# RWKV systems in two PSUM banks, TensorE's order beside r, v and z written out by hand, mixed inputs in other slots, next weights handed over

## The chip, the cores and the metric

The kernel runs on one core of one Trainium2 chip. The metric is the device time of one execution in microseconds (us); the time of a kernel is the median over several executions. Engines are named as in the profile: PE is TensorE (PEld its weight loads), DVE is VectorE, ACT is ScalarE, POOL is GpSimd, SP is the engine whose queue issues the DMAs.

## The reference

One inference step of two layers over 1104 tokens (8 sequences of 8, 16 meta tokens, 1024 of a prompt) with 1024 channels, all in fp32. Layer 0 is a gated DeltaNet, layer 1 RWKV-7 time mixing. The change lies in layer 1, in what comes before its recurrence:

```
xx = xprev - xn
xs = xn[None] + xx[None] * mu[:, None, None, :]
rkvz = jnp.einsum('sbtd,sde->sbte', xs[:4], w_rkvz)
...
kk = l2norm((k * k_k).reshape(B, T, H, N))
...
S = (S * d_t[:, :, None, :]
     + jnp.einsum('bhvk,bhk->bhv', S, -kk_t)[..., None] * b_t[:, :, None, :]
     + v_t[..., None] * k_t[:, :, None, :])
```

So every one of r, k, v, z is a 1024 x 1024 projection of its own mixture of a token and the token before it. The kernel does the recurrence in chunks of 64 tokens; for each chunk and head the effect of the kk and b terms is a lower triangular system, whose inverse it needs. Those inverses need only k, the decay and the rate a, so that they can be worked out while r, v and z are still being projected.

## The kernel before, in words

**Stages of layer 1.** First keys, decays and rates (`keys_decay_rate`, L1134: for each of 8 output tiles k the key projection, then two small second projections, `lora_second`). Then the stage of the change (`layer1`, L1861): 24 projections in the order r, v, z with 8 output tiles of 128 channels each, and beside them 24 systems in 5 batches. Then `wave` (L1905), which runs the recurrence over 24 items with the last third of the tokens' z projection, the output projection and the last norm beside it.

**A projection.** The tokens lie in three segments of 384, 384 and 336 (`SEGS`). Operands are split in two parts, high and low, so that a product takes three matmuls (high x high, low weight x high, high weight x low). One segment of one output tile is 8 input tiles x 3 = 24 matmuls into one PSUM tile (`dense`, L236, tag "d", 4 buffers). ACT copies the result out (L1131; for z ACT and DVE gate it, L1003) and SP stores it. r and v take three segments, z two; the third of z waits for the wave.

**Weights.** `load_w` (L195) loads half an output tile's weights, 4 x 128 x 128, as `wraw` (2 buffers); `split` (L82) then has ACT write the high part `whi` (L86) and POOL the low part `wlo` (L90). whi and wlo have three buffers each, and a projection holds two of them, so that the second half of the next projection can be split only when the first half of this one has been read for the last time, after matmul 12 of 24 of its last segment.

**Mixed inputs.** For each of r, v and z, `mix` has `mix_part` (L1028) make 8 input tiles x its segments: `mix_raw` (L1032) is one ACT and one DVE instruction (two each in the first segment), then ACT writes the high part and, for odd k POOL, for even k DVE, the low part (L90). They lie in 11 slots: r in 0 to 5, 9, 10, v in 6, 7, 8, 0, 1, 2, 9, 10, z in 3 to 10. The keys before used 3 to 10. So for v three of the slots are free beforehand, and the rest are freed by the last projection of r, segment by segment. The names of the tiles in the profile are xa, xc, xh and xl; they show the slot, not the part.

**Systems.** `rwkv_inverse` (L1272) does one batch of 4 or 5 items. For each item: a load (`sldcak`), three ACT functions (two exponentials, a square), three products (L1290 and L1296 on DVE, L1295 on POOL), 48 small matmuls into `fL` and 8 into `frss`, copied out by ACT (L1306, L1308) and a DVE transpose (L1322). For the batch: `inverse32` (L457) builds a 32 x 32 inverse in each partition, 31 steps of two DVE instructions (L470, L472) of 31 to 256 elements each, in the SBUF tile `invT` that POOL has zeroed (L461) and given its diagonal (L465). Two DVE transposes (L1336 `T1n`, L1337 `sTD`) follow. Then for each item `merge_left` (24 small matmuls into `mY`, two ACT copies L484) and `merge_right` (24 into `mU`, two ACT copies); both take PSUM tag "m", two buffers. At last the batch is stored (L1344).

**What sets the order.** The queue of each engine is written by a planner when the program is built: it takes the instructions as far as possible in the order in which they are traced and by its own estimate of when their inputs are ready. Once written, a queue is executed in order. In `layer1` projections and batches are traced one after the other (batches after projections 0, 3, 6, 9, 12), and the planner alone puts the small matmuls of the systems between those of the projections. The wave stands in `manual_schedule` for PE and ACT, which keeps the traced order on these. Its weights come from `stream` (L217), which keeps up to six halves loaded ahead and three split.

## Time and profile before

| what | us |
|---|---|
| time, median of 3 | 2294.88 (2293.03 to 2296.75) |
| the profiled execution's own time | 2294.9 |
| its span, first to last instruction | 2293.2 |
| PE busy in the span | 2142.2 (93%) |
| DVE busy | 1591.0 (69%) |
| ACT busy | 1270.4 (55%) |
| POOL busy | 926.3 (40%) |

How to read it: the span is 1.7 us shorter than the execution that it belongs to. The stage of the change is the stretch from about 1481 us, where r's projections begin in earnest, to about 1860 us, where the wave's first matmuls (`zz`) begin. A row of "windows" gives a stretch, its length, then for PE, PEld, DVE, ACT and POOL the busy time and in brackets the number of instructions, then the granted TensorE clock (1.00 is full), the busy share of the DMA engines and GB/s. A row of groups gives line, engine, operation, tiles and shape, the count, the busy time of the group and the mean duration of one in ns, then the idle time before them and what ended it. A row of waits gives who waited for whom: total us, number of times, longest. Neighbouring matmuls overlap in the records, so that what counts is the distance from start to start.

### The profile page before, as it was taken

The numbers are of one execution on the slowest core, as the hardware profiler recorded it, in microseconds if no ns is written. First come the engines' busy times: TensorE is split into PE (matmuls) and PEld (weight loads), VectorE is DVE, ScalarE is ACT, GpSimd is POOL, SyncE is SP. The second block draws the span as 40 slices with busy tenths as digits, with TensorE's granted clock in tenths as the row PEclk, the third lists the DMA queues.
The fourth block names the chain that finished last, engine by engine and source line by source line (L and its number), as shares of the span: only waits on it lengthen the run. The fifth ranks groups of instructions, "written<-read, shape, count | busy, mean of one in ns | idle before, by whom it ended". The sixth has DMA issues, their size and how long they took to land. (4 is left out here: it accounts for less than half of the span.)

```text
span 2293.2 us, 55145 instructions
## 1 busy us (share of the span) xinstructions
PE 2142.2 (93%) x20452; PEld 1957.5 (85%) x20452; DVE 1591.0 (69%) x4222; ACT 1270.4 (55%) x3638; POOL 926.3 (40%) x1263
## 2 busy tenths in 40 slices
PE   5989999989999999999999998999889899999997
PEld 5888988989898998988998998898778888888786
DVE  6878769585868769586334765768977737776655
ACT  5445556555555556465534464664744436677674
POOL 3435344443434344443321352364533444444444
PEclk9999999999999999999999999999989999999999
DMA  4324232323334232335435225565444375677754
GB/s 117 101 77 109 75 96 79 104 83 88 102 90 108 67 105 73 102 89 156 122 89 156 72 63 188 194 201 155 149 140 135 90 212 156 192 212 228 226 164 143
DMA packets 430663, 292.66 MB, mean 128 GB/s; under 512 B 147146, under 2 KB 412987, under 8 KB 430395
## 3 DMA queue, kind: packets, MB, share of 16 engines
q1 hardware_dynamic: 430394, 289.14, 44.1%
q8 instruction: 161, 2.64, 0.5%
q14 instruction: 108, 0.88, 0.1%
HBM read 197.68 MB, written 91.37 MB: 126 GB/s over the span
## 5 line engine op out<-in xcount | busy, mean ns | idle before, releaser
L90 POOL TENSOR_TENSOR wlo<-wraw,whi 128x512 fp32r<-128x512 f32 (+1 forms) x246 | 325.5, 1326 | 379.1 <-ACT whi L86 366.9
L76 PE MATMUL d<-xc,whi 128*128 128x384 f32 (+2 forms) x910 | 263.7, 346 | 4.7 <-DVE key L1187 2.3
L86 ACT CAST whi<-wraw 128x512 fp32r<-128x512 f32 (+1 forms) x246 | 150.2, 613 | 105.1 <-PE dq L76 50.6
L434 DVE SCALAR_TENSOR_TENSOR cvy<-raw,cw,cvy 128x408 f32<-128x408 f32 (+2 forms) x288 | 179.4, 636 | 16.3 <-ACT cvy L62 14.5
L76 PEld LDWEIGHTS d<-xc,whi 128*128 128x128 f32 (+1 forms) x910 | 171.2, 195 | 12.0 <-issue 3.9
L472 DVE TENSOR_TENSOR invT<-invT,invtmp 72x31 f32<-72x31 f32 (+31 forms) x403 | 174.1, 432 | 6.7
L470 DVE TENSOR_TENSOR invtmp<-invA,invT 72x31 f32<-72x31 f32 (+31 forms) x403 | 164.4, 408 | 12.2 <-DMA invA<-ltd 5.4
L76 PE MATMUL dz<-xc,whi 128*128 128x384 f32 (+1 forms) x480 | 149.8, 343 | 0.0
L76 PE MATMUL dv<-xc,whi 128*128 128x384 f32 (+1 forms) x480 | 146.7, 335 | 0.0
L76 PE MATMUL d<-xc,wlo 128*128 128x384 f32 (+2 forms) x428 | 146.2, 347 | 0.2
L76 PE MATMUL d<-xa,whi 128*128 128x384 f32 (+3 forms) x450 | 140.6, 346 | 2.3 <-DVE xa L90 0.9
L834 POOL TENSOR_SCALAR Sb<-Sb,eglb 128x128 f32<-128x128 f32 x128 | 80.1, 643 | 88.2 <-DMA Sb<-in_state_gdn 43.8
L76 PE MATMUL dz<-xa,whi 128*128 128x384 f32 (+1 forms) x288 | 101.5, 352 | 0.0
L76 PE MATMUL dv<-xa,whi 128*128 128x384 f32 (+1 forms) x288 | 100.4, 349 | 0.1
L76 PEld LDWEIGHTS dz<-xc,whi 128*128 128x128 f32 x480 | 90.1, 193 | 0.8
L76 PEld LDWEIGHTS d<-xa,whi 128*128 128x128 f32 (+1 forms) x450 | 84.5, 192 | 6.7 <-issue 2.4
L76 PEld LDWEIGHTS dv<-xc,whi 128*128 128x128 f32 x480 | 88.5, 188 | 0.5 <-issue 0.4
L76 PE MATMUL d<-xl,whi 128*128 128x384 f32 (+1 forms) x256 | 84.7, 347 | 3.2 <-DVE xl L90 1.7
L62 ACT ACTIVATE o<-rA,gcol 128x128 f32<-128x128 f32 x128 | 46.6, 372 | 73.2 <-DVE S L745 72.5
L76 PE MATMUL d<-xh,wlo 128*128 128x384 f32 (+1 forms) x256 | 85.0, 346 | 1.7 <-POOL wlo L90 1.7
L76 PE MATMUL d<-xa,wlo 128*128 128x384 f32 (+3 forms) x252 | 85.6, 340 | 0.0
L62 ACT ACTIVATE attn<-attn,gcol 128x128 f32<-128x128 f32 x144 | 46.5, 390 | 70.2 <-POOL attn L545 70.1
(518 smaller groups left out, 7022.9 us busy)
## 6 DMA issues: line engine op xcount, KB each, us to landing
wraw<-in_gdn_w_in SPq DMA_DIRECT2D x96, 256.0 KB
wraw<-in_rwkv_w_rkvz SPq DMA_DIRECT2D x80, 256.0 KB
Sb<-in_state_gdn SPq DMA_DIRECT2D x64, 256.0 KB
sldcak<-cakd SPq DMA_DIRECT2D x24, 576.0 KB
cakd<-ev SPq DMA_DIRECT2D x56, 192.0 KB
wraw<-in_rwkv_w_o SPq DMA_DIRECT2D x42, 256.0 KB
E<-drow SPq DMA_DIRECT2D x24, 384.0 KB
attn<-drow SPq DMA_DIRECT2D x24, 384.0 KB
```

The lines of the kernel that those rows point to most:

```text
L62: return self.nc.scalar.activation(out, in_, func, bias=bias, scale=scale, **kw)
L76: self.nc.tensor.matmul(out, lhsT, rhs, start=start, stop=stop)
L86: nc.scalar.copy(hi, x)
L90: e.tensor_tensor(lo, x, hi.bitcast(F32), op=ALU.subtract)
L434: nc.vector.scalar_tensor_tensor(y[:, 0:wd], raw[:, k:k + wd], cw[k], y[:, 0:wd], op0=ALU.mult, op1=ALU.add)
L470: nc.vector.tensor_tensor(tmp, A[:, j, j + 1:32].unsqueeze(2).broadcast_to([nb, n, m]), Tv[:, j, 0:m].unsqueeze(1).broadcast_to([nb, n, m] ...
L472: nc.vector.tensor_tensor(Tv[:, j + 1:32, 0:m], Tv[:, j + 1:32, 0:m], tmp, op=ALU.subtract)
L834: nc.gpsimd.tensor_scalar(Sb[:, u], Sb[:, u], self.eglb[:, hv, 4 * g + u:4 * g + u + 1], None, op0=ALU.mult)
```

## The change

- **The inverse grows in PSUM.** `inverse_steps` replaces `inverse32` for these five batches: the tile T of 128 x 1024 lies in PSUM (tag "T", one buffer, as wide as two of the 512-wide PSUM tiles) in place of SBUF, DVE zeroes it and writes the diagonal in place of POOL, and after each of the 31 steps the generator yields. With it tag "d" has 3 buffers in place of 4 in this stage and tag "m" 1 in place of 2, and the PSUM pool is opened anew after the keys.
- **TensorE's order is written out.** The stage stands in `manual_schedule` for PE. `projections` yields after every 8 matmuls: 64 segments x 3 = 192 places. What is to be traced at a place stands in `plan`: item n's small matmuls (`lower`) and the loads and products of item n + 1 (`prepare`) at place `LOWER[n]`; the steps of batch b's inverse spread over the places up to `END[b]`; the left merge of its item q at `END[b] + 2 + 3q`, the right merge two places later. The other engines stay with the planner.
- **Mixed inputs in other slots.** r takes slots 0, 1, 3 to 7, 2; v 8, 9, 10, 0, 1, 3, 4, 2; z 5 to 10, 3, 4. `free` says how many of a projection's first inputs lie in slots that the projections before it do not use: 2 for r, 3 for v and z. Those are mixed during keys 2 to 4 (r) or tiles 4 to 6 of the matrix before (v, z), the others behind each segment of its last tile; for this the last tile of the keys is done segment by segment. The first tile of a matrix begins with the matmuls of its free inputs for all segments and then returns to finish each segment. All low parts are made by POOL.
- **Next weights handed over.** The weights of the next projection are loaded half by half, behind the first and the last segment. The wave's first z tile finds its weights split (projection 24 in `weights`) and those of the second loaded (`raws`); `stream` takes both.

No matmul is added or left out. The diff, without parts that only move or repeat lines:

```diff
-    def stream(self, srcs):
-
-        raw, w = [], []
+    def stream(self, srcs, first, loaded):
+
+        raw, w = [None] * len(first) + loaded, list(first)
         for n in range(len(srcs)):
-            while len(raw) < min(n + 6, len(srcs)):
+            while len(raw) < min(n + 6 - (n == 1), len(srcs)):
                 q = len(raw)
                 if q > 2 and len(w) < q - 2:
                     x, m, c = raw[len(w)]
                     hi, lo = (self.t(self.wp, [128, 4, 128], a, 3, F32R) for a in ("whi", "wlo"))
                     self.split(x[:, 0:m, 0:c], hi[:, 0:m, 0:c], lo[:, 0:m, 0:c])
...
-                raw.append(self.load_w(srcs[q], srcs[q].shape[0] // 128, later=True, pool=self.fin if q % 3 == 2 else None))
-            while len(w) < min(n + 3, len(srcs)):
+                raw.append(self.load_w(srcs[q], srcs[q].shape[0] // 128, later=True, pool=self.fin if q % 3 == 1 else None))
+            while len(w) < min(n + 3 - (n == 1), len(srcs)):
...
-        p = self.ps("m", 2, "Y")
+        p = self.ps("m", 1, "Y")
...
-        p = self.ps("m", 2, "U")
+        p = self.ps("m", 1, "U")
...
-    def mix_part(self, m, k, a, b, xb, xh, xl, pool):
+    def mix_part(self, m, k, a, b, xb, xh, xl, pool, lo=None):
         x = self.mix_raw(m, k, a, b, xb, pool)
-        self.split(x, xh[:, a:b], xl[:, a:b], eng_lo="pool" if k % 2 else "dve")
+        self.split(x, xh[:, a:b], xl[:, a:b], eng_lo=lo or ("pool" if k % 2 else "dve"))
...
-                for (c0, n), p in zip(SEGS, self.projected(1, k, x, k in (0,))):
+                for s, ((c0, n), p) in enumerate(zip(SEGS, self.projected(1, k, x, k in (0, 7)))):
...
+                    if k == 7:
+                        behind(s)
                 self.lora_second(0, k, hh, w2, dst_w)
                 self.lora_second(1, k, hl, w2, dst_a)
+                between(k)
 
...
-    def rwkv_inverse(self, b, pool):
-
-        items = range(max(5 * b - 1, 0), 5 * b + 4)
+    def inverse_steps(self, A, pool, diag, e):
+
+        self.uid += 1
+        T = self.pp.tile([128, 1024], F32, name=f"invT_{self.uid}", tag="T", bufs=1)
+        self.nc.vector.memset(T, 0.0)
+        self.nc.vector.tensor_copy(T[:, 0:1024:33], diag)
+        Tv = T.rearrange("p (i j) -> p i j", j=32)
+        for j in range(31):
+            n, m = 31 - j, j + 1
+            tmp = self.t(pool, [128, 256], "invtmp", 1)[:, 0:n * m].rearrange("p (n m) -> p n m", m=m)
+            e.tensor_tensor(tmp, A[:, j, j + 1:32].unsqueeze(2).broadcast_to([128, n, m]),
+                            Tv[:, j, 0:m].unsqueeze(1).broadcast_to([128, n, m]), op=ALU.mult)
+            e.tensor_tensor(Tv[:, j + 1:32, 0:m], Tv[:, j + 1:32, 0:m], tmp, op=ALU.subtract)
+            yield
+        return Tv
+
+    def inverse_plan(self, pool):
+
         nc, t = self.nc, self.t
-        rk2, L21, GD, TD = self.rk2[:, b], self.L21[b % 2], self.GD, self.TD
-        for q, n in enumerate(items):
+        keep = {}
+        GD, TD = self.GD, self.TD
+
+        def prepare(n):
             s, p = divmod(n, 8)
-            C = slice(6 * q, 6 * q + 6)
...
+            keep[n] = sq, bk, al
+
+        def lower(b, q, n):
+            s, p = divmod(n, 8)
+            sq, bk, al = keep.pop(n)
+            C = slice(6 * q, 6 * q + 6)
+            rk2, L21 = self.rk2[:, b], self.L21[b % 2]
             gp = self.ps("f", 2, "L")
...
+        def chain(b):
+            rk2 = self.rk2[:, b]
+            nc.vector.reciprocal(rk2, rk2)
+            blk = t(pool, [128, 32], "bblk", 1)
+            nc.vector.transpose(blk, rk2)
+            A = t(pool, [128, 32, 32], "invA", 1)
+            flat = lambda x: x.rearrange("p a b -> p (a b)")
+            nc.vector.transpose(flat(A), flat(GD))
+            nc.vector.tensor_tensor(A, A, blk.unsqueeze(2).broadcast_to([128, 32, 32]), op=ALU.mult)
+            Tv = yield from self.inverse_steps(A.rearrange("p i s -> p s i"), pool, blk, nc.vector)
+            T1n = t(pool, [128, 32, 32], "T1n", 1)
+            if b == 0:
+                for a in (32, 96):
+                    nc.gpsimd.memset(TD[a:a + 32, :, 1, :], 0.0)
+            nc.vector.transpose(T1n.rearrange("p c j -> p j c"), Tv.rearrange("p i j -> p j i"))
+            nc.vector.transpose(TD[:, :, 0, :].rearrange("p c i -> p i c"), Tv)
+            keep["T", b] = T1n
+        def left(b, q):
             C = slice(6 * q, 6 * q + 6)
-            self.merge_right(self.merge_left(L21[:, C], T1n[:, C], pool), TD[:, C])
-        w = 6 * len(items)
-        d = self.ttd[b].rearrange("s (c x i) -> s c x i", x=2, i=32)[:, 0:w]
-        for a in (0, 64):
-            nc.sync.dma_start(d[a:a + 32], TD[a:a + 32, 0:w])
-            for x in (0, 1):
-                nc.sync.dma_start(d[a + 32:a + 64, :, x], TD[a + 32:a + 64, 0:w, 1 - x])
+            keep["Y", b, q] = self.merge_left(self.L21[b % 2][:, C], keep["T", b][:, C], pool)
+        def right(b, q):
+            self.merge_right(keep.pop(("Y", b, q)), TD[:, 6 * q:6 * q + 6])
+        def store(b, items):
+            w = 6 * len(items)
+            d = self.ttd[b].rearrange("s (c x i) -> s c x i", x=2, i=32)[:, 0:w]
+            for a in (0, 64):
+                nc.sync.dma_start(d[a:a + 32], TD[a:a + 32, 0:w])
+                for x in (0, 1):
+                    nc.sync.dma_start(d[a + 32:a + 64, :, x], TD[a + 32:a + 64, 0:w, 1 - x])
+        return prepare, lower, chain, left, right, store
...
-        self.keys_decay_rate(x, self.hh, self.hl)
+        todo = [(m, k) for m in (0, 2, 3) for k in range(8)]
+        order = {0: (0, 1, 3, 4, 5, 6, 7, 2), 2: (8, 9, 10, 0, 1, 3, 4, 2), 3: (5, 6, 7, 8, 9, 10, 3, 4)}
+        free = {0: 2, 2: 3, 3: 3}
+        segs = {0: 3, 2: 3, 3: 2}
+        lows = {0: "pool", 2: "pool", 3: "pool"}
+        W = {}
+        def part(m, k, s):
+            c0, n = SEGS[s]
+            self.mix_part(m, k, c0, c0 + n, xb[k], *self.slots[order[m][k]], self.ev, lows[m])
+        def weights(n, h, elo=None):
+            if n < 25:
+                m, k = (todo + [(3, 0)])[n]
+                (hi,), (lo,) = self.load_w(self.i["rwkv_w_rkvz"][0, m][512 * h:512 * h + 512, 128 * k:128 * k + 128], 4, elo=elo)
+                W[n, h] = hi, lo
+        def between(k):
+            if k in (2, 3, 4):
+                for q in range(free[0]):
+                    part(0, q, k - 2)
+        def behind(s):
+            if s != 1:
+                weights(0, s // 2)
+            for q in range(free[0], 7):
+                part(0, q, s)
+        self.keys_decay_rate(x, self.hh, self.hl, between, behind)
+        for s in range(3):
+            part(0, 7, s)
+        self.psum_pool()
         ip = pool("rinv", ctx)
         self.rwkv_masks(ip, True)
-        todo = [(m, k) for m in (0, 2, 3) for k in range(8)]
-        slots = {0: (0, 1, 2, 3, 4, 5, 9, 10), 2: (6, 7, 8, 0, 1, 2, 9, 10), 3: range(3, 11)}
-        for n, (m, k) in enumerate(todo):
-            if k == 0:
-                x = self.mix(m, xb, slots[m], SEGS[0:2] if m == 3 else SEGS)
-            self.project(m, k, x, {0: self.rd, 2: self.vd, 3: self.zd}[m], k in range(8))
-            if n in (0, 3, 6, 9, 12):
-                self.rwkv_inverse((0, 3, 6, 9, 12).index(n), ip)
-            if n == 16:
-                zin = self.gate_inputs(xa, xb)
+        prepare, lower, chain, first_, second_, store = self.inverse_plan(ip)
+        plan = {}
+        at = lambda u, f, *a: plan.setdefault(u, []).append((f, a))
+        LOWER = (13, 17, 21, 25, 29, 33, 38, 43, 48, 53, 60, 67, 73, 79, 85, 90, 95, 100, 104, 110, 118, 126, 134, 142)
+        DUR, END = (0,), (49, 80, 105, 143, 170)
+        runs = [[chain(b), 0] for b in range(5)]
+        def pump(b, f):
+            while runs[b][1] < f:
+                runs[b][1] += 1
+                next(runs[b][0], None)
+        at(0, prepare, 0)
+        for b in range(5):
+            items = range(max(5 * b - 1, 0), 5 * b + 4)
+            for q, n in enumerate(items):
+                at(LOWER[n], lower, b, q, n)
+                if n < 23:
+                    at(LOWER[n], prepare, n + 1)
+            u0 = LOWER[items[-1]] + 1
+            if b:
+                u0 = max(u0, END[b - 1] + 1)
+            for u in range(u0, END[b] + 1):
+                at(u, pump, b, 99 if u == END[b] else 33 * (u + 1 - u0) / (END[b] + 1 - u0))
+            for q in range(len(items)):
+                at(END[b] + 2 + 3 * q, first_, b, q)
+                at(END[b] + 2 + 3 * q + 2, second_, b, q)
+            at(END[b] + 2 + 3 * q + 2, store, b, items)
+        def projections():
+            for n, (m, k) in enumerate(todo):
+                ps = {}
+                f = free[m] if k == 0 else 0
+                for first, s in [(True, s) for s in range(segs[m] if f else 0)] + [(False, s) for s in range(segs[m])]:
+                    c0, w = SEGS[s]
+                    if s not in ps:
+                        ps[s] = self.ps("d", 3)
+                    p = ps[s]
+                    for c in range(0 if first else 3 * f, 3 * f if first else 24):
+                        q, j = divmod(c, 3)
+                        xh, xl = self.slots[order[m][q]]
+                        hi, lo = W[n, q // 4]
+                        l, r = ((hi, xh), (lo, xh), (hi, xl))[j]
+                        self.mm(p[:, 0:w], l[:, q % 4], r[:, c0:c0 + w], start=c == 0, stop=c == 23)
+                        if c % 8 == 7 and c < 23:
+                            yield
+                    if first:
+                        continue
+                    late = b_now[0] in ()
+                    if s == 0:
+                        weights(n + 1, 0, "dve" if late else None)
+                    if s == segs[m] - 1:
+                        weights(n + 1, 1, "dve" if late else None)
+                    f_ = t(self.ev, [128, 384], "ev", 3)
+                    if m == 3:
+                        self.gate(f_[:, 0:w], p[:, 0:w])
+                    else:
+                        nc.scalar.copy(f_[:, 0:w], p[:, 0:w])
+                    nc.sync.dma_start({0: self.rd, 2: self.vd, 3: self.zd}[m][k][:, c0:c0 + w], f_[:, 0:w])
+                    nm = {0: 2, 2: 3}.get(m)
+                    if nm:
+                        if 4 <= k < 7 and k - 4 < segs[nm]:
+                            part(nm, s, k - 4)
+                        if k == 7 and s < segs[nm]:
+                            for q in range(free[nm], 8):
+                                part(nm, q, s)
+                    yield
+        b_now = [-1]
+        t = self.t
+        with tc.manual_schedule(engines={mybir.EngineType.PE}):
+            for u, _ in enumerate(projections()):
+                b_now[0] = max([b for b in range(5) if u > LOWER[max(5 * b + 3, 0)]], default=-1)
+                for f, a in plan.pop(u, ()):
+                    f(*a)
+                if u == 146:
+                    zin = self.gate_inputs(xa, xb)
+            raws = [self.load_w(self.i["rwkv_w_rkvz"][0, 3][512 * h:512 * h + 512, 128:256], 4, later=True) for h in (0, 1)]
+            for u in sorted(plan):
+                for f, a in plan.pop(u):
+                    f(*a)
...
-            self.wave(zin, stay, last, pool)
+            self.wave(zin, [W[24, h] for h in (0, 1)], raws, stay, last, pool)
```

25 lines of the change are left out of this document (5 added, 20 removed).

## Prediction

> **What bounds the kernel now.** First the windows by stage: the stage of the change and the wave's first 15 us.
>
> ```profile
> 1481.00:1860.00 379.00, 345.30 (x4019) 317.59 (x4020) 291.89 (x548) 200.25 (x490) 164.02 (x224) 0.93 0.51 153
> 1860.00:1875.00 15.00, 11.62 (x62) 10.37 (x61) 2.76 (x7) 4.23 (x9) 5.98 (x5) 0.77 0.75 218
> ```
>
> TensorE bounds the stage: 345.3 of 379 us busy, 33.7 idle. Its granted clock is 0.93 there. What that costs is seen in the chain (22 matmuls of z at full clock, the row before them 21 behind a gap) in two narrow windows, and in the gap between these from the timeline.
>
> ```profile
> 1816.57 5.01 PE d L76 x21
> 1822.37 4.06 PE d L76 x22
> ...
> 1622.00:1625.00 3.00, 3.00 (x19) 3.00 (x18) 2.93 (x8) 2.17 (x6) 1.05 (x3) 1.00 0.53 163
> 1628.00:1631.00 3.00, 3.00 (x53) 2.40 (x45) 2.96 (x7) 1.68 (x4) 2.03 (x3) 0.50 0.49 182
> 1627.73 1.06 PE L76 MATMUL fL<-sldcak 64*32 64x64 f32 x41 [2.37 <-issue]
> ```
>
> A matmul takes 0.185 us at full clock (4.06 / 22). The clock is 1.00 or 0.50; the first window lies ahead of the gap of 2.37 us, the second behind it. A mean of 0.93 is half clock for 14% of the stage (0.07 / 0.5), and 14% of 345.3 busy us, at half speed, lose 24 us. So the same matmuls without a gap would take 379 - 33.7 - 24 = **321 us**, and each us of gap costs 0.71 us more in clock (24 / 33.7).
>
> Then the waits of TensorE, 1481 to 1870 us:
>
> ```profile
> PE fL L76 <- DVE sldcak L1296: 11.0, 8, 2.4
> PE mY L76 <- DVE T1n L1336: 6.8, 3, 3.1
> PE zz L76 <- DVE zst L1003: 3.2, 1, 3.2
> PE fL L76 <- ACT sldcak L62: 2.8, 2, 1.5
> PE fL L76 <- issue: 2.4, 1, 2.4
> PE mU L76 <- ACT invY L484: 2.0, 3, 0.9
> ```
>
> Most of the gaps, 25.0 us in the five rows of fL, mY and mU, stand before small matmuls of the systems, which the planner put where their inputs were not ready yet, mostly behind DVE. That leaves 8.7 of 33.7 for all else. Why DVE is late is seen in its timeline, with POOL's row of the same time below:
>
> ```profile
> 1801.98 1.48 DVE L470 TENSOR_TENSOR invtmp<-invA,invT 128x220 f32<-128x220 f32 x1
> 1803.50 1.35 DVE L472 TENSOR_TENSOR invT<-invT,invtmp 128x220 f32<-128x220 f32 x1
> 1804.89 0.37 DVE L470 TENSOR_TENSOR invtmp<-invA,invT 128x207 f32<-128x207 f32 x1
> ...
> 1801.61 3.00 POOL L90 TENSOR_TENSOR wlo<-wraw,whi 128x512 fp32r<-128x512 f32 x2 [1.53 <-issue]
> ```
>
> While POOL splits weights, a step of the inverse takes 1.4 us; the next, hardly smaller, takes 0.37.
>
> **Part 1, the inverse in PSUM.** One view gives minimum, median and maximum of the steps, the mixing (both tensors in SBUF) and the gate (one in PSUM); the group rows give totals.
>
> ```profile
> L470 DVE TENSOR_TENSOR invtmp<-invA,invT x155: 176/374/1548, 1536.5 to 1813.2; 128x31 f32<-128x31 f32 x10, 128x60 f32<-128x60 f32 x10, 128x87 f32<-128x87 f32 x10, 128x112 f32<-128x112 f32 x10
> L470 DVE TENSOR_TENSOR invtmp<-invA,invT 128x31 f32<-128x31 f32 (+15 forms) x155 | 70.1, 453 | 4.0
> L472 DVE TENSOR_TENSOR invT<-invT,invtmp 128x31 f32<-128x31 f32 (+15 forms) x155 | 73.8, 476 | 3.9
> L1044 DVE SCALAR_TENSOR_TENSOR mixs<-xb,pcol,mixs x60: 536/578/1650, 1481.1 to 1799.2; 128x336 f32<-128x336 f32 x24, 128x384 f32<-128x384 f32 x20, 128x320 f32<-128x320 f32 x16
> L1003 DVE SCALAR_TENSOR_TENSOR ev<-ev,d x16: 524/551/556, 1791.1 to 1861.3; 128x384 f32<-128x384 f32 x16
> L461 POOL MEMSET invT<- 128x1024 f32 x5 | 4.8, 953 | 15.3 <-DVE sTD L1337 15.3
> L465 POOL COPY invT<-bblk 128x32 f32<-128x32 f32 x5 | 5.3, 1064 | 1.4 <-DVE bblk L1326 1.4
> L1336 DVE STREAM_TRANSPOSE T1n<-invT 128x1024 f32<-128x1024 f32 x5 | 10.6, 2117 | 0.1
> ```
>
> L1003 never passes 556 ns, L470 and L1044 reach 1548 and 1650. With T in PSUM both step instructions have one input there, so I take all 310 at L470's median, 374 ns: 116 us in place of 143.9 (70.1 + 73.8), **28 us of DVE time saved**, 5.6 per batch. No row has DVE writing PSUM. Bounds: the collisions stay (nothing saved), or the steps fall to the minimum, 176 ns (89 us saved); the gate, nearest in kind, is as long with PSUM as the mixing's shortest without, so the median stands. Zeroing and diagonal pass from POOL to DVE, taken at POOL's rows: 2.0 us per batch. A batch then holds DVE for 62 x 0.374 + 2.0 and four passes over 1024 elements, each at most like T1n's 2.1: 34 us.
>
> [...]
>
> **Part 2, the order beside it.** No matmul goes, so 321 us is the floor and the question is which gaps remain. The rows that fill the places:
>
> ```profile
> L76 PE MATMUL fL<-sldcak 64*32 64x32 f32 (+1 forms) x1152 | 24.4, 218 | 18.2 <-DVE sldcak L1296 11.0 <-ACT sldcak L62 2.8 <-issue 2.4
> L76 PE MATMUL frss<-ssq,hones 64*32 64x192 f32 x192 | 18.3, 367 | 0.0
> L1044 DVE SCALAR_TENSOR_TENSOR mixs<-xb,pcol,mixs 128x336 f32<-128x336 f32 (+2 forms) x60 | 46.1, 777 | 1.4 <-ACT mixs L62 1.3
> L1296 DVE TENSOR_TENSOR sldcak<-sldcak 128x384 f32<-128x384 f32 x24 | 15.1, 627 | 9.5 <-POOL sldcak L1295 9.5
> L1295 POOL TENSOR_TENSOR sldcak<-sldcak 128x384 f32<-128x384 f32 x24 | 26.1, 1086 | 5.3 <-ACT ssq L62 4.0
> L90 POOL TENSOR_TENSOR wlo<-wraw,whi 128x512 fp32r<-128x512 f32 x46 | 62.8, 1366 | 71.5 <-ACT whi L86 66.4 <-issue 2.8 <-PE d L76 1.9
> L90 POOL TENSOR_TENSOR xa<-mixs,xa 128x336 fp32r<-128x336 f32 (+1 forms) x11 | 11.4, 1038 | 8.0 <-ACT xa L86 8.0
> L90 POOL TENSOR_TENSOR xl<-mixs,xh 128x384 fp32r<-128x384 f32 (+1 forms) x9 | 13.3, 1482 | 12.8 <-ACT xh L86 12.8
> L62 ACT ACTIVATE sTD<-mU 32x192 f32<-32x192 f32 x48 | 15.3, 319 | 23.0 <-PE mU L76 22.6
> L86 ACT CAST whi<-wraw 128x512 fp32r<-128x512 f32 x46 | 28.4, 617 | 8.2 <-PE d L76 3.4 <-DMA wraw<-in_rwkv_w_rkvz 3.3 <-issue 1.3
> ```
>
> A place is 8 matmuls, 1.48 us; an item's fL and frss add at most (24.4 + 18.3) / 24 = 1.8 us.
>
> - **fL.** The items' products are traced 4 to 8 places, 6 to 12 us, ahead of their matmuls, and take 2 x 0.63 us on DVE and 1.09 on POOL. The 11.0 + 2.8 + 2.4 us go: 0 left.
> - **mY.** The left merge stands in TensorE's queue two places behind `END`; if T1n is late, all behind it waits. Batch 0 has 24 places and 5 items, 44 us, against 34 + 5 x 1.7 + 2 of mixing = 45 us of DVE; batch 1 31 places, 55 us, against 34 + 9 + 18 x 0.78 = 57; batch 4 27 places, 40 us, against 34 + 9 gates x 0.55 + 5 x 0.78 = 43. Batches 2 and 3 have room (46 against 43, 65 against 55). I take 2 us for each of the three crowded ones: 6.
> - **Turn from r to v.** Five inputs per segment are mixed behind r's last tile, all low parts now on POOL, at 1.04 to 1.48 us, say 1.18: 15 x 1.18 + 3 wlo + 2 L1295 = 24 us. TensorE has until then 2 segments, 27 matmuls on free inputs, 42 of the second pass and 2 items: 117 x 0.185 + 3.6 = 25. Even: 3 us. From v to z, 10 inputs: 16 against 19: 1 us. From the keys to r, 18 inputs, begun one segment earlier: 2 us, about as now.
> - **Weights.** The second half can be split after matmul 12 of the last segment and is needed 24 matmuls, 4.4 us, later; ACT and POOL need 2.0 (0.62 and 1.37). Two POOL instructions ahead of it eat the rest. 0.1 us each: 2.
> - **One bank for Y and U.** A left merge follows a right one by one place, 1.48 us, in which ACT empties the bank (2 x 0.32) behind at most one or two others: 1 us; at worst 19 x 0.6.
> - **Taken at nothing.** Six mixtures of r move into keys 2 to 4; they feed nothing that TensorE reads before r. Three buffers of tag "d" for four: a tile is wanted again two segments, 8 us, after its last matmul, and ACT's copy takes under 0.5 (bound: one copy's wait at each of 64 segments, were ACT 8 us behind). One tile T: the next batch starts after `END` in any case. SP issues the same loads and stores; only the items' loads stand elsewhere, a whole item ahead of their use. The PSUM pool opened anew makes r's first tiles wait for the keys' copies: in the 2 us above.
>
> Together 15 us of gap, 25.6 with the clock: the stage takes 321 + 25.6 = 346.6, **32.4 us less**.
>
> **Part 3, the weights handed over.** The wave's first window loses 3.4 us idle and, at half clock for 46%, 2.7 more. The chain there, and the recurrence's first loads:
>
> ```profile
> 1860.20 5.04 DMA wraw<-in_rwkv_w_rkvz
> 1867.40 2.05 PE zz L76 x6
> ...
> 1840.86 0.57 PE L76 MATMUL mU<-sTD,invY 32*32 32x32 f32 x24
> 1844.73 0.42 SPq L1254 DMA_DIRECT2D fld2c<-cakd  x1
> 1851.18 0.55 DVE L1372 TENSOR_TENSOR AR<-fldrv,fDp 128x384 f32<-128x384 f32 x1
> ```
>
> The waits name DVE, but the chain shows the second tile's weights: landed at 1865.2, behind the recurrence's loads in SP's queue. They now come earlier. What is late next: those loads follow the last merge (1841.4) and have their operands ready 10 us later. Before, z went on for 18 us behind that merge; now 5 places, 7 us, so they are ready 3 us into the wave, and wanted after 30 matmuls, 5 us. Of 6.1 us I take **4**; bounds 0 and 6.
>
> **Sum.** The profiled execution took 2294.9 us (span 2293.2 and 1.7 around it), the median of the runs. 2294.9 - 32.4 - 4 = **2258.5 us**, 1.6% faster.
>
> **Rivals.**
> - *No gap is left.* 2294.9 - 58 - 6 = 2231. For it: fL's inputs have long leads. Against: three batches without room.
> - *The written order waits as the planner's does*, so that the change does not do what it says: DVE, ACT and POOL still stand in the planner's order. With 27 us of gap, as much as the systems' now, the stage takes 321 + 46, and the time is 2279.
> - *Steps no cheaper in PSUM*, so that the 5.6 us per batch are not saved: the three crowded batches come 5.6 us later, 17 x 1.71 = 29 us: 2287. The gate's row speaks against it. [...]
> - *Slower, through POOL.* Each wlo of a second half must pass within 2.4 us. If the low parts (32 more on POOL, 38 us) and L1295 stand ahead of it in the order, TensorE halts in every projection. From 2.7 us of loss in each of 24 (64 / 24) all is lost; at 3 us, with the clock's part, the time is 2294.9 - 64 + 72 = 2303. For it: a queue in fixed order cannot step aside. Against: POOL would be busy (164 + 38 - 10) / 347, 55%.
>
> **How the numbers follow.** Forecast (2246 to 2272) 0.52; no gap 0.08; planner-like 0.16; dear steps 0.05; within 0.2% (4.6 us, about what a measurement of this kernel tells from no change) 0.05; slower 0.14. Faster 0.81. The range 2234 to 2300 leaves out the slower case and some of the gapless one, 0.19.
>
> **What would show it.** The steps' maximum near their median, none over 0.6 us; no wait of fL over 1 us; mY's waits at batches 0, 1, 4 alone; stage clock 0.96 or more; zz without the 3.2 us wait. Wrong if TensorE waits for POOL's wlo or xl over 10 us in all, or if T1n comes late at every batch.

## The result and the profile after

The changed kernel takes 2295.84 us (median of 14 runs, 2290.99 to 2298.76), the kernel before 2294.90 (14 runs) beside it: a ratio of 1.0003, 95% interval 0.9992 to 1.0014. **No change**, where 2258.5 was forecast. The profiled execution took 2295.8 us, its span is 2294.1.

The windows of the changed kernel that answer the first two of before:

```profile
1481.00:1860.00 379.00, 345.46 (x4037) 313.99 (x4037) 252.50 (x525) 199.11 (x482) 172.98 (x235) 0.94 0.50 149
1860.00:1875.00 15.00, 13.13 (x109) 11.90 (x110) 4.61 (x11) 4.82 (x10) 6.48 (x10) 0.90 1.13 326
```

VectorE's busy time fell from 291.9 to 252.5 us, and TensorE is busy as long as before, over the same 379 us. The steps of the inverse (minimum, median, maximum in ns):

```profile
L1285 DVE TENSOR_TENSOR invtmp<-invA,invT x155: 172/354/421, 1544.8 to 1814.0; 128x31 f32<-128x31 f32 x10, 128x60 f32<-128x60 f32 x10, 128x87 f32<-128x87 f32 x10, 128x112 f32<-128x112 f32 x10
L1287 DVE TENSOR_TENSOR invT<-invT,invtmp x155: 185/366/433, 1545.0 to 1814.2; 128x31 f32<-128x31 f32 x10, 128x60 f32<-128x60 f32 x10, 128x87 f32<-128x87 f32 x10, 128x112 f32<-128x112 f32 x10
```

No step is longer than 0.433 us, where one was 1.55; all 310 take 105.6 us. The longest waits of TensorE, 1481 to 1870 us:

```profile
PE mU L76 <- ACT invY L484: 7.9, 4, 3.7
PE d L76 <- POOL wlo L90: 6.8, 3, 3.4
PE mY L76 <- ACT sTD L62: 6.7, 4, 3.0
PE zz L76 <- DVE ev L1003: 2.7, 1, 2.7
PE d L76 <- ACT ev L2000: 2.6, 2, 2.1
PE fL L76 <- issue: 2.3, 2, 2.1
PE d L76 <- ACT whi L86: 1.9, 2, 1.5
PE fL L76 <- ACT sldcak L62: 1.8, 1, 1.8
```

VectorE's two large rows are gone (fL 11.0, T1n 6.8). In their place TensorE waits for ScalarE's copies of Y and U, 14.6 us. And the stage begins later; first the longest waits from 1440 to 1515 us in the changed kernel, then in the one before:

```profile
PE flora L76 <- ACT ev L62: 9.1, 5, 6.6
PE d L76 <- POOL wlo L90: 3.4, 1, 3.4
PE d L76 <- ACT ev L2000: 2.1, 1, 2.1
PE d L76 <- ACT whi L86: 1.5, 1, 1.5
```

```profile
PE flora L76 <- ACT ev L62: 1.2, 2, 1.0
PE d L76 <- DVE xa L90: 0.9, 1, 0.9
```

The longest wait of the last second projections of the keys' stage (`flora`), 6.6 us, is seen in ScalarE's timeline of the changed kernel:

```profile
1475.43 0.52 ACT L62 ACTIVATE ev<-d,pcol 128x336 f32<-128x336 f32 x1
1477.98 0.47 ACT L86 CAST xc<-mixs 128x336 fp32r<-128x336 f32 x1 [2.02 <-DVE mixs L1044]
1478.35 0.57 ACT L62 ACTIVATE ev<-flora,pcol 128x384 f32<-128x384 f32 x1
```

The copy that frees flora's bank stands behind r's mixing, and that waits 2.0 of these 6.6 us for VectorE.

**Stretches.** The time at which the keys' stage is reached differs from run to run by some us (VectorE copies the keys' tile 3 at 1410 to 1424 us). So the runs are compared by stretches between instructions that all of them have, read from the trace: A, the turn, from the start of VectorE's copy of the keys' tile 3 (first segment) to that of ScalarE's copy of r's tile 1 (last segment); B, from there to ScalarE's last copy of z; C, from there to zz's first matmul; D, zz's first 48; E, the rest.

| kernel | time, ratio (95%) | A | B | C | D | E |
|---|---|---|---|---|---|---|
| before | 1 | 94.4 | 347.9 | -0.9 | 22.2 | 411.0 |
| changed | 1.0003 (0.9992 to 1.0014) | 106.7 | 336.3 | 2.0 | 18.4 | 415.7 |
| t_psum_alone | 0.9931 (0.9905 to 0.9958) | 99.0 | 317.8 | 5.4 | 22.6 | 413.8 |
| t_psum_handover | 0.9917 (0.9893 to 0.9941) | 99.1 | 320.3 | 1.1 | 22.2 | 411.7 |
| planner_order | 0.9991 (0.9977 to 1.0005) | 104.5 | 329.4 | 4.8 | 24.0 | 411.6 |
| whole_inverses | 0.9926 (0.9902 to 0.9949) | 105.1 | 318.2 | 1.1 | 18.2 | 420.1 |
| whole_late | 0.9910 (0.9879 to 0.9941) | 99.2 | 311.9 | 1.1 | 27.0 | 415.0 |
| u_later | 0.9969 (0.9953 to 0.9985) | 107.5 | 325.8 | 1.1 | 22.0 | 415.4 |
| fixed_best | 0.9928 (0.9902 to 0.9954) | 98.7 | 322.4 | 1.1 | 23.1 | 417.9 |
| room_alone | 1.0054 (1.0033 to 1.0075) | 98.5 | 336.8 | 7.9 | 22.4 | 419.4 |

A to E are of one profiled execution each; E varies from 410 to 420 us over all versions, with no order that fits their changes, which is why a few us in a stretch don't always show in the ratio. Beside the kernel before, the changed one loses 12.3 us in A, gains 11.6 in B, loses 2.9 in C, gains 3.8 in D, and E is 4.7 longer; its A began 3.6 us earlier, so that the two spans differ by 0.9 us.

### The profile page after: what moved, and what is told of

Same layout as the page of the kernel before. It is cut to its first block, busy times and chain, and to the rows that moved or that the text cites. A ratio compares the mean times of both kernels' runs of the same rounds, so it can differ in the third digit from the quotient of the medians.

```text
span 2294.1 us, 55205 instructions
## 1 busy us (share of the span) xinstructions
PE 2133.1 (93%) x20452; PEld 1943.4 (85%) x20452; DVE 1558.2 (68%) x4200; ACT 1273.9 (56%) x3638; POOL 949.9 (41%) x1285
## 4 chain that ended last, share of the span: by engine, by line
PE 53%; DVE 15%; DMA 9%; ACT 8%; POOL 5%; issue 5%; SPq 1%; DVEq 0%; POOLq 0%; ACTq 0%
PE d L76 16%; PE dz L76 6%; PE rA L76 4%; PE dk L76 4%; PE dq L76 3%; DVE invT L472 2%; DVE invtmp L470 2%; DMA attn<-drow 2%; PE rX L80 2%; DVE cvy L434 1%; PE do L76 1%; POOL attn L545 1%; DMA sldcak<-cakd 1%; PE fG L76 1%; PE zz L76 1%
## 5 line engine op out<-in xcount | busy, mean ns | idle before, releaser
L76 PE MATMUL d<-xc,whi 128*128 128x384 f32 (+2 forms) x1006 | 287.6, 343 | 4.0 <-ACT whi L86 2.1
L76 PEld LDWEIGHTS d<-xc,whi 128*128 128x128 f32 (+1 forms) x1006 | 186.6, 192 | 8.8 <-ACT whi L86 2.9
L76 PE MATMUL d<-xc,wlo 128*128 128x384 f32 (+3 forms) x476 | 163.5, 347 | 6.8 <-POOL wlo L90 6.8
L76 PEld LDWEIGHTS d<-xc,wlo 128*128 128x128 f32 (+1 forms) x476 | 91.3, 192 | 11.8 <-POOL wlo L90 7.8
L472 DVE TENSOR_TENSOR invT<-invT,invtmp 72x31 f32<-72x31 f32 (+15 forms) x248 | 99.0, 399 | 2.8
L470 DVE TENSOR_TENSOR invtmp<-invA,invT 72x31 f32<-72x31 f32 (+15 forms) x248 | 96.0, 387 | 7.2 <-DMA invA<-ltd 4.4
L1044 DVE SCALAR_TENSOR_TENSOR mixs<-xb,pcol,mixs 128x320 f32<-128x320 f32 (+2 forms) x96 | 78.3, 823 | 15.3 <-ACT mixs L62 14.6
```

Source lines behind the costliest of these rows:

```text
L76: self.nc.tensor.matmul(out, lhsT, rhs, start=start, stop=stop)
L470: nc.vector.tensor_tensor(tmp, A[:, j, j + 1:32].unsqueeze(2).broadcast_to([nb, n, m]), Tv[:, j, 0:m].unsqueeze(1).broadcast_to([nb, n, m] ...
L472: nc.vector.tensor_tensor(Tv[:, j + 1:32, 0:m], Tv[:, j + 1:32, 0:m], tmp, op=ALU.subtract)
L1044: nc.vector.scalar_tensor_tensor(x[:, f:], xb[:, 8 + a + f:8 + b], mu, x[:, f:], op0=ALU.mult, op1=ALU.add)
```

## The experiments

**The first four** take one part each out of the changed kernel. *Low parts to both engines:*

```diff
-        lows = {0: "pool", 2: "pool", 3: "pool"}
+        lows = {0: None, 2: None, 3: None}
```

> The changed kernel with one edit: the low parts of the mixed inputs of r, v and z go to POOL and DVE in turn, as in the kernel before, instead of all to POOL. Theory A (the gain of the steps is lost at the turn from the keys to r, where the mixing of r's inputs stands ahead of the keys' own copies in ACT's and DVE's queues, and in TensorE's fixed places that wait for ACT): TensorE's waits for POOL's wlo and low parts go, some 5 us, the turn's 11 us stay, since the mixing stays where it is: 2291 us (2287 to 2295). Theory B (POOL, which does every low part, is what is late and what slows DVE): the 11 us of the turn, the 3.5 us of wlo and half of the places' 14 us go: 2278 us (2272 to 2284).

Ratio 0.9988 (0.9970 to 1.0005); A 102.3, B 334.7. That is theory A's size in the time: POOL is not the main cause, though A is 4.4 us shorter, where theory A had the turn stay.

*r's mixing behind the keys:*

```diff
         def behind(s):
             if s != 1:
                 weights(0, s // 2)
-            for q in range(free[0], 7):
-                part(0, q, s)
...
         for s in range(3):
-            part(0, 7, s)
+            for q in range(free[0], 8):
+                part(0, q, s)
```

> The changed kernel with one edit: r's inputs 2 to 6 are mixed behind the whole of the keys, decays and rates, not within the last tile of the keys; weights and the two free inputs stay as they are. Theory A: the 9 us that TensorE waits for the copies of the last keys' banks go, r's inputs come as late as in the kernel before, where r's first product was 10.9 us earlier; r's tile 1 then waits for the rest of the mixing, so that half of it comes back: 2290 us (2284 to 2295), and no wait of the decays' and rates' products for ACT over 2 us. Theory B (POOL's low parts set r's start): r's second tile starts no earlier than now and the time stays: 2296 us (2293 to 2300).

Ratio 0.9979 (0.9960 to 0.9998); A is 102.0 in place of 106.7. The turn's waits in this run:

```profile
PE flora L76 <- ACT ev L62: 6.5, 5, 3.6
PE d L76 <- POOL xa L90: 1.9, 1, 1.9
PE d L76 <- POOL wlo L90: 0.9, 1, 0.9
```

The place of the mixing costs some 5 us, as theory A has it; but flora still waits 6.5 us, 3.6 of them at once, where no wait over 2 was expected, so something else stands there too.

*T in SBUF again:*

```diff
-        T = self.pp.tile([128, 1024], F32, name=f"invT_{self.uid}", tag="T", bufs=1)
+        T = self.t(pool, [128, 1024], "invT", 1)
```

> The changed kernel with one edit: the growing inverse T is a tile of SBUF again, all else (order of TensorE, places, slots, handover) stays. The steps go from 105.6 us to about 144 us of VectorE. Theory A (VectorE is not what is late; ACT's queue and the turn are): T1n still comes ahead of its places, since each batch has 24 to 38 places of 1.8 us for 29 us of steps: 2298 us (2295 to 2302), TensorE's longest wait for T1n under 3 us. Rival (the shorter steps are what keeps the fixed places on time): VectorE is 77% busy again and T1n and the copies behind it are late at every batch, 3 to 6 us each: 2312 us (2305 to 2325).

Ratio 1.0044 (1.0027 to 1.0061), 9 us behind the changed kernel, between the two; B 341.7, and no wait for T1n. In the written order only 9 us come out of the shorter steps.

*TensorE's order to the planner:*

```diff
-        with tc.manual_schedule(engines={mybir.EngineType.PE}):
+        with ExitStack():
```

> The changed kernel with one edit: TensorE's order in the stage of r, v and z and the inverses is left to the planner again; T in PSUM, the mixing, the slots and the handover stay. Theory A (the turn and ACT's queue): r's first products pass the products of decays and rates that wait, the merges are put later, but the planner brings back waits of its own at the same size as in the kernel before, now without the late T1n: 2290 us (2283 to 2298). Rival C (the written order itself is what costs, since nothing passes a waiting product): the 11 us of the turn and the 14 us at the places of Y and U go: 2272 us (2262 to 2280).

Ratio 0.9991; B is 7 us shorter, A 2. Rival C falls in its size: the written order is not most of the loss.

**Four on the places and on part 1.** *Y and U further apart:* `END[b] + 2 + 3 * q` becomes `END[b] + 2 + 4 * q`, for Y, U and the store.

> The changed kernel with one edit: the places of the products for Y and U of one batch lie four places apart from item to item, not three, so that each use of their one bank has two places of some 1.8 us to be copied out, where Y had one. Theory A (ACT's copy out of the one bank of Y and U is waited for at fixed places): mY's waits for ACT, 6.7 us in the changed kernel, fall under 2.5 us, mU's 7.9 us stay, since U still comes two places behind Y: 2292 us (2288 to 2296). Theory D (these waits only stand in for TensorE time that would be lost at the next place anyway, since ACT is behind as a whole): the waits turn up at other tiles, the stage is as long: 2296 us (2292 to 2299).

Ratio 1.0013 (0.9992 to 1.0035), yet B falls to 329.3 us, and mY's wait to 2.8, while mU's rises to 9.5. The gain in B is as theory A has it; the time doesn't show it, and the profiled run reached the keys' tile 3 nearly 9 us later than the changed kernel's.

*The copies of Y and U first:* both merges are traced in `with self.tc.high_priority():`.

> The changed kernel with one edit: the copies of Y and U out of their bank go ahead of the other work in ACT's queue (high priority for what the merges trace), TensorE's order unchanged. Theory A (these copies stand in ACT's queue behind exponentials that wait for an item's load, and behind the mixing): mU's and mY's waits, 14.6 us in the changed kernel, fall to 5 us or less: 2287 us (2283 to 2292). Theory D (ACT is behind as a whole): what was ahead of the copies comes later, and the products of the lower blocks or the mixed inputs wait instead: 2296 us (2291 to 2300).

Ratio 1.0004 (0.9985 to 1.0024), B 337.0, mU and mY 14.6 us as in the changed kernel. But in the two traces ScalarE runs the stage in the same order, from 1481 to 1850 us, except for one copy of Y that stands one instruction earlier. So the edit did not put the copies first, and the run speaks neither for theory A nor against it.

*Three edits:* mix_behind_keys, lows_both and merges_apart at once.

> The changed kernel with three edits at once: r's inputs 2 to 6 mixed behind the keys, decays and rates; low parts to POOL and DVE in turn; the places of Y and U four apart. If the causes are separate, their gains at the end of the stage add up: 6.3 us (zz's first product with the mixing moved) and 2.3 us (with the low parts in turn) and some 4 us of mY's waits, 12.6 us: 2283 us (2279 to 2288), the first version ahead of both kernels by more than the scatter. Theory D (one engine behind as a whole, whatever is moved): no more than the best of the three alone, 2290 us (2287 to 2294).

Ratio 0.9975 (0.9958 to 0.9993); A 98.6, B 331.6. The turn's gains add up; those in B do not.

*Part 1 alone, in the kernel before:*

```diff
-        T = self.t(pool, [128, 1024], "invT", 1)[0:nb]
-        nc.gpsimd.memset(T, 0.0)
...
-            nc.gpsimd.tensor_copy(T[:, 0:1024:33], diag)
...
+            T = self.pp.tile([128, 1024], F32, name=f"invT_{self.uid}", tag="T", bufs=1)
+            nc.vector.memset(T, 0.0)
+            nc.vector.tensor_copy(T[:, 0:1024:33], diag)
...
-        p = self.ps("m", 2, "Y")
+        p = self.ps("m", 1, "Y")
...
-        p = self.ps("m", 2, "U")
+        p = self.ps("m", 1, "U")
...
-        return (self.dense(w, 128, *x, s, bufs=4) for s ...
+        return (self.dense(w, 128, *x, s, bufs=4 if m == 1 else 3) for s ...
...
         self.keys_decay_rate(x, self.hh, self.hl)
+        self.psum_pool()
```

> The kernel before with the first part of the change alone: T in two PSUM banks (Y and U then share one bank, the products of r, v and z have three, and PSUM is given out anew behind the keys); the planner orders TensorE, nothing is fixed, handed over or mixed elsewhere. Theory A (T in PSUM gives its 38 us of VectorE back in the late T1n, 18 us of waits for products of the lower blocks and T1n): 2284 us (2278 to 2290). Theory E (T in PSUM helps only where the fixed places use the time; the planner's order keeps its waits): 2294 us (2290 to 2299). Slower, if the copy of the last keys is waited for at the new layout of PSUM and the one bank of Y and U costs each merge: 2303 us.

Ratio 0.9931 (0.9905 to 0.9958), **15.8 us faster by the ratio**, 12.4 by the medians (2278.49 beside 2290.87): theory A, at the fast end of its range. So the first part of the change is the gain, and the other parts give it all back. B of the kernel before, of this run and of the changed kernel, each as one window, with TensorE's busy time first:

```profile
1512.90:1860.80 347.90, 316.14 (x3824) 290.38 (x3824) 263.85 (x503) 174.62 (x433) 141.05 (x190) 0.93 0.49 149
```

```profile
1512.50:1830.30 317.80, 305.95 (x3832) 280.85 (x3828) 222.91 (x507) 173.34 (x427) 127.17 (x176) 0.98 0.49 150
```

```profile
1521.60:1857.90 336.30, 312.43 (x3815) 283.84 (x3805) 223.91 (x484) 170.99 (x420) 144.07 (x193) 0.96 0.48 145
```

31.8 us idle before, 11.9 with T alone, 23.9 in the changed kernel; the clock was 0.93, 0.98 and 0.96. The planner, given shorter steps, left only these waits in B (t_psum_alone):

```profile
PE mY L76 <- DVE T1n L1339: 8.8, 3, 4.0
PE d L76 <- DVE invT L475: 2.0, 1, 2.0
PE d L76 <- POOL wlo L90: 1.1, 1, 1.1
```

**Four on what gives it back.** Three of the expectations that follow (pieces_planner, whole_inverses, u_later) count their stretch from the beginning of r's tile 1 on TensorE, 9 to 13 us ahead of B: 345.0 us for the changed kernel's B of 336.3, 342.2 for the 329.4 of planner_order, 326.6 for the 317.8 of T alone. So what is compared is the difference from the run that was edited.

*T and the handover, nothing else:* t_psum_alone with `stream`, `first` and `raws` of the change.

> The kernel before with two parts of the change: T in two PSUM banks and the handover of the first gate tile's split weights and of the next two raw blocks; the planner orders TensorE, the mixing and the slots are those of before. Theory A (the handover is worth the 4 us that the changed kernel shows between zz's first and its 48th product, and keeps them where nothing else moves): 2274 us (2270 to 2279) beside 2278.5 for T alone. Theory F (what the gate's fill gains is taken back in the chain of the wave): 2278 us (2275 to 2283).

Ratio 0.9917 (0.9893 to 0.9941). C is 4.3 us shorter, but D is not, and B is 2.5 longer; beside T alone's 0.9931 the intervals overlap. Its worth isn't settled.

*Pieces, with the planner's order and the mixing of before:* planner_order with `order` and `lows` as before the change and all of a matrix mixed at its first tile.

> The changed kernel with TensorE's order left to the planner and with the mixing of r, v and z as in the kernel before (at each matrix's first tile, its slots, low parts in turn); the inverses are still traced in pieces, place by place, and the handover stays. T in PSUM alone went from tile 1 of r to the end of z in 326.6 us, the changed kernel with the planner's order in 342.2. Theory P (it is the tracing in pieces, which puts each item's exponentials, products and copies behind whatever was traced before them on ACT and DVE): 340 us of that stretch (335 to 346), 2288 us. Theory M (it is the early mixing with its low parts on POOL): 328 us (324 to 333), 2276 us.

Ratio 0.9960 (0.9941 to 0.9978); A 96.8, B 327.5, beside planner_order 7.7 us less in A and 1.9 in B: the mixing of before restores the turn, not B.

*Whole inverses, with the planner's order and the mixing of the change:*

```diff
-                at(LOWER[n], lower, b, q, n)
-                if n < 23:
-                    at(LOWER[n], prepare, n + 1)
+                at(u, prepare, n)
+                at(u, lower, b, q, n)
...
-            for u in range(u0, END[b] + 1):
-                at(u, pump, b, 99 if u == END[b] else 33 * (u + 1 - u0) / (END[b] + 1 - u0))
+            at(u, pump, b, 99)
```

Here u is 8, 35, 62, 89 and 116 for the five batches, and the merges stand at u too.

> The changed kernel with TensorE's order left to the planner and each batch's inverse traced as a whole behind r's and v's tiles 0, 3, 6, 9 and 12, as in the kernel before; the early mixing with its low parts on POOL, the slots and the handover stay. Theory P (tracing in pieces is what costs in the stretch from tile 1 of r to the end of z): 329 us of that stretch (325 to 334), the turn from the keys to r as late as in the changed kernel, 2279 us. Theory M (the mixing): 341 us (336 to 346), 2291 us.

Ratio 0.9926 (0.9902 to 0.9949); B 318.2, A 105.1. **Theory P holds** (11.2 us of B gone, 13 forecast): with the planner's order, tracing in pieces costs 11 us of B, the mixing 8 us of A, and they are separate.

*U five places behind Y, in the lower blocks' banks:*

```diff
-        p = self.ps("m", 1, "U")
+        p = self.ps("f", 2, "U")
...
-                at(END[b] + 2 + 3 * q + 2, second_, b, q)
+                at(END[b] + 2 + 3 * q + 5, second_, b, q)
```

> The changed kernel with its fixed order of TensorE, but U's products go into the two banks of the lower blocks and stand five places behind Y's, not two in the same bank. Theory A (ACT's copies come up to 4 us behind the place, no more): mU's and mY's waits for ACT, 14.6 us, fall under 4 us, and the stretch from tile 1 of r to the end of z takes 334 us (330 to 338) in place of 345.0: 2285 us (2281 to 2290). Theory D (the waits move on to the lower blocks' products and the mixed inputs, since the work of ACT and DVE for an item comes late as a whole): 341 us or more, 2292 us (2289 to 2297).

Ratio 0.9969 (0.9953 to 0.9985); B 325.8 in place of 336.3, A 107.5. Its longest waits in B:

```profile
PE d L76 <- POOL wlo L90: 6.8, 5, 2.3
PE mY L76 <- ACT invY L484: 4.6, 3, 2.9
```

Theory A holds for B: the waits for the copies of Y and U fall from 14.6 to 4.6 us, those for wlo grow from 3.5 to 6.8, and B is 10.5 us shorter. In the written order the places of Y and U, with the one bank that they share, cost these 10 us; merges_apart, which moves places alone, took 7.0 from B.

**Four to add up.** *Only the items whole:* whole_inverses, with the steps spread over the 24 places behind each batch's items and the merges behind them.

> As whole_inverses (planner's order, early mixing, handover), but only the items of a batch are traced as a whole behind tiles 0, 3, 6, 9 and 12; the inverse's steps are spread over the next 24 places and Y and U stand three places apart behind them, as in the changed kernel. From ScalarE's copy of the end of r's tile 1 to its last copy of z, whole_inverses took 318.2 us and the planner's order with all in pieces 329.4. If the items' pieces cost the 11 us (each item's exponentials, products and copies come only one item ahead of their place): 319 us (316 to 323), 2278 us. If the spread steps and merges cost them: 328 us (325 to 332), 2288 us.

Ratio 0.9930 (0.9904 to 0.9955), B 319.2: it is the items' pieces that cost the planner, not the steps' or the merges'.

*The best of the planner's order:* whole_inverses with the edits of lows_both and mix_behind_keys.

> whole_inverses with two more edits: r's inputs 2 to 6 mixed behind the keys, decays and rates, and low parts to POOL and DVE in turn. If the causes add up: the turn is shorter by the 8 us that three_edits had there against the changed kernel (r's tile 1 copied 98.6 us after the copy of the keys' tile 3, in place of 105.0), the rest stays at 318 us: 2271 us (2266 to 2276), ahead of all versions so far. If the planner had already moved this work out of the way: 2277 us (2273 to 2281).

Ratio 0.9910 (0.9879 to 0.9941), 2273.11 us median beside 2291.21: **the lowest ratio of all, ahead of both kernels.** A is 5.9 us shorter than in whole_inverses, B 6.3, D 8.8 longer. Its interval overlaps with those of T alone, t_psum_handover, whole_inverses, items_whole and fixed_best, so that the order among these isn't settled.

*The best of the written order:* the changed kernel with the edits of u_later, lows_both and mix_behind_keys.

> The changed kernel with its fixed order and pieces, and three edits: U in the lower blocks' banks five places behind Y, r's inputs 2 to 6 mixed behind the keys, low parts in turn. If the turn and ACT's copies at the places are all that the fixed order lost: the 8 us of the turn and the 10 us of u_later add up: 2278 us (2274 to 2283), as good as T alone. If the pieces themselves hold VectorE's and ScalarE's work back: 2284 us (2281 to 2289).

Ratio 0.9928 (0.9902 to 0.9954); A 98.7, B 322.4. The causes add up in the written order too; it comes level with T alone (0.9931), pieces and all.

*The room without T:* t_psum_alone with T left in SBUF.

> The kernel before with the room for T made in PSUM and not used: PSUM given out anew behind the keys, three banks for r, v and z, one for Y and U, T in SBUF as before. It measures what the room costs by itself. T alone had r's tile 1 copied 99.0 us after the copy of the keys' tile 3, the kernel before 94.4. If that 4.6 us is the room's price at the turn and the one bank for Y and U costs nothing: 2299 us (2295 to 2303). If the bank costs what the prediction had as its bound, 11 us: 2309 us. If the room is free and the 4.6 us are chance: 2294 us.

Ratio 1.0054 (1.0033 to 1.0075), **12 us slower**. Its longest waits, 1465 to 1870 us:

```profile
PE zz L76 <- ACT whi L86: 7.9, 1, 7.9
PE mY L76 <- DVE T1n L1336: 6.9, 5, 2.7
PE flora L76 <- ACT ev L62: 5.1, 3, 4.4
```

flora's wait comes with the room made in PSUM, without any early mixing: this is what mix_behind_keys left. Otherwise the trace doesn't show the price: A is 4.1 us longer than in the kernel before and zz waits 7.9 us in C, but B is 11.1 us shorter (336.8), with T in SBUF as before. So of the 30.1 us that T alone gains in B, only 19.0 are seen against the room alone. The profiled run took 2297.5 us, and 7 of the 12 runs 2305 to 2315; where their time lies stays open.

**Two on what holds Y's copy back.** The changed kernel's timeline around the first long wait (SPq is the DMA queue):

```profile
1582.51 0.89 SPq L1382 DMA_DIRECT2D ttd<-sTD  x2
1583.50 0.52 SPq L1257 DMA_DIRECT2D sldcak<-cakd  x1
...
1588.15 1.08 ACT L62 ACTIVATE sldcak<-sldcak 128x383 f32<-128x383 f32 x2 [5.46 <-DMA sldcak<-cakd]
1589.24 0.63 ACT L484 COPY invY<-mY 32x192 f32<-32x192 f32 x2
...
1589.92 0.78 PE L76 MATMUL mU<-sTD,invY 32*32 32x32 f32 x24 [3.37 <-ACT invY L484]
```

In the DMA queue's own waits, 1565 to 1592 us:

```profile
SPq L1382 <- DVE sTD L1366: 4.2, 1, 4.2
```

An item's load is issued behind the stores of the batch's result, which wait for the transpose sTD; ScalarE waits for the load with the item's exponentials, and Y's copy and then TensorE stand behind them. Ahead of four of the eight waits for copies of Y and U ScalarE has run an item's exponentials, after standing idle for 2.4 to 5.6 us; these four make 8.3 of the 14.6 us, the longest, 3.7, among them. The other four, 6.2 us, fall into the mixing of v and z, as here:

```profile
1656.12 0.51 ACT L86 CAST xc<-mixs 128x384 fp32r<-128x384 f32 x1 [0.68 <-DVE mixs L1044]
1656.98 0.80 ACT L62 ACTIVATE mixs<-xb,omu 128x64 f32<-128x64 f32 x2 [0.34 <-POOL xc L90]
1657.68 0.64 ACT L62 ACTIVATE sTD<-mU 32x192 f32<-32x192 f32 x2
1658.37 0.85 PE L76 MATMUL mY<-T1n,L 32*32 32x32 f32 x24 [2.45 <-ACT sTD L62]
```

*VectorE copies Y and U:* `nc.vector.tensor_copy` and `nc.vector.tensor_scalar` in the merges.

> The changed kernel with one edit: VectorE, not ScalarE, copies Y and U out of their bank; order of TensorE, places, pieces and the one bank stay. In the changed kernel ScalarE stands 40.7 us waiting for the items' loads from r's tile 1 to the end of z, 12 times, and TensorE 14.6 us waiting for ScalarE's copies of Y and U. If it is those loads that hold the copies back (they stand behind the exponentials in one queue): the waits for Y and U fall to 5 us or less, the stretch from 336.3 to 327 us (323 to 331), 2286 us. If any engine that does them is late, since the places are too close: the waits stay, now for VectorE, the stretch is 336 us or more, 2295 us.

Ratio 1.0017 (1.0002 to 1.0032), B 336.5, and mU and mY wait 19.0 us, now for VectorE: the second outcome by its numbers. Its timeline at the same place:

```profile
1587.93 1.08 ACT L62 ACTIVATE sldcak<-sldcak 128x383 f32<-128x383 f32 x2 [6.68 <-DMA sldcak<-cakd]
...
1588.48 0.56 DVE L1309 TENSOR_TENSOR sldcak<-sldcak 128x383 f32<-128x383 f32 x1 [1.35 <-ACT sldcak L62]
1589.07 0.73 DVE L484 COPY invY<-mY 32x192 f32<-32x192 f32 x2
...
1589.94 0.85 PE L76 MATMUL mU<-sTD,invY 32*32 32x32 f32 x24 [4.83 <-DVE invY L484]
```

The copy stands behind the same item here as well, by way of its product. The edit did not take the load out of the way, so the run does not tell the two apart. *ScalarE in the traced order too:* Activation is added to the engines of `manual_schedule`.

> The changed kernel with one edit: in the stage of r, v, z and the inverses ScalarE keeps the traced order too, as TensorE does, in place of the planner's. In the changed kernel the planner put an item's exponentials ahead of the copies of Y, because by its estimate the item's load had landed; the load came 5.5 us later (issued behind a waiting store), and TensorE waited 3.4 us for Y's copy; VectorE, which did the copies in another run, stood behind the same item's product. If this place in the queue is the cause: the 14.6 us of waits for Y and U fall to 5 us or less, the stretch from r's tile 1 to the end of z from 336.3 to 327 us (323 to 331), 2286 us. If a fixed order of ScalarE as well only hands the waiting on (the split weights and the mixing then stand behind copies that wait for TensorE): 340 us or more, 2300 us.

Ratio 1.0112 (1.0086 to 1.0137), 26 us slower. Waits, 1440 to 1870 us:

```profile
PE d L76 <- ACT ev L2000: 14.1, 3, 7.3
PE mY L76 <- ACT sTD L62: 11.7, 3, 10.4
PE d L76 <- ACT whi L86: 8.2, 1, 8.2
```

mU's wait fell to 4.3 us, but ScalarE now stands in the mixing and waits for VectorE (1512 to 1860 us: 22.5 us ahead of xc, 21.1 of xh, 16.5 of xa), with the projections' copies behind it, for which TensorE waits 14.1 us. What holds the copies back in the changed kernel is thus seen in the trace, not isolated by a run; that more room between Y and U takes most of the wait away is shown by u_later.

## Why the prediction was wrong

- **Part 1 was right on VectorE, its term too small.** 28 us of VectorE time forecast, 38.3 measured (143.9 - 105.6): no step passes 0.433 us. The gate's row spoke more clearly than the prediction took it: the mixing's 536 ns is of a 128 x 320 row, and at the gate's width, 128 x 384, the mixing never falls below 585 in the kernel before. What the shorter steps are worth depends on the order. The third rival puts them at 29 us; in the written order they bring 9 (t_in_sbuf against the changed kernel), in the planner's order some 28 (T alone against the room alone, 0.9931 / 1.0054 = 0.988).
- **The turn from the keys to r failed.** "About as now", 2 us; it is 12.3 longer in A. I counted how long 18 inputs take beside TensorE's work and not what they stand ahead of: the copies out of the banks of flora and d. In A the room's part is 4.6 (T alone against before) and that of the mixing and its low parts 8.1 (three_edits against the changed kernel).
- **The places of Y and U failed.** 1 us of ScalarE's lateness forecast, with "at most one or two others" ahead of a copy; 14.6 measured. A mean distance in places says little when one copy stands behind an item's load and TensorE waits 3.7 us for it. u_later takes 10.5 us of B away.
- **The room for T failed as a step.** I took the PSUM pool opened anew as part of 2 us and the one bank as 1, with 11 as the bound. In the order of the kernel before the room costs 12 us by itself (0.33 to 0.75%). In the changed kernel it was not measured apart, and part of it is the one bank for Y and U, counted above.
- **fL and T1n.** fL's three rows fell from 16.2 us to 4.1, where 0 was forecast (a fourth row, 2.1 us behind the step L472, stands in none of its sums for fL). T1n was feared in vain, 6 us at batches 0, 1 and 4: no wait at all. A batch's steps, zeroing and diagonal took 22.2 us in place of 25.2, more than the 1 to 2 us by which it was reckoned late; that this is the reason is not shown apart.
- **The turns from r to v and v to z** have next to no waits of their own, and POOL's wlo holds TensorE for 3.5 us in B; 6 were forecast for the two turns and the weights. But 6.2 of the 14.6 us of Y and U fall into the mixing of these turns.
- **z's end had no term.** z's last gate came late, and zz waits 2.7 us for it (C).
- **Part 3 isn't shown.** D is 3.8 us shorter, 4 forecast, but C is 2.9 longer: from ScalarE's last copy of z to zz's 49th matmul 20.4 us for 21.3. In u_later, with the same handover and zz not held up (C 1.1), D is 22.0 as in the kernel before.
- **The frame held.** B of the changed kernel against T alone: 18.5 us for 12.0 us of idle time, 1.5 us per us of gap, where I took 1.71.
- **The rivals.** "The written order waits as the planner's does" came nearest in its mechanism, with 27 us of gap for the 23.9 in B; its time was 2279. The measured time lies within 0.2%, a case that had a chance of 0.05 and no mechanism. The slower case did not come: POOL's wlo costs 6.8 us from 1481 to 1870 us, under the 10 that were named. Of the signs, the steps' maximum came (0.433 us); fL still waits up to 2.1 us, and the stage's clock is 0.94, not 0.96. The range 2234 to 2300 holds the time only because it was that wide.

All in all, the waits that the change was to remove were mostly removed by part 1 alone: the planner with short steps has 11.9 us of idle time in B. Parts 2 to 4 together put back 12.0 us of idle time there and 8 us at the turn. In B it is the items traced in pieces (items_whole, in the planner's order) and the places of Y and U (u_later, in the written order); at the turn it is the mixing.

## What to carry to other kernels

Try the parts of a change apart: here one part gains 0.7% and the others give it back. In an order written out by hand, leave each product as many places as the worst wait of the engine that feeds it, not as its mean; and of work moved earlier, ask whose copies it now stands ahead of. A resource that is made room for (here two PSUM banks) has a price, here 12 us, that is measured by making the room without using it.
